# FFN's second projection on one Trainium2 core: product 5 in one row, and the sums for products 6 and 3 on product 7's weight tile

## The chip, the cores and the metric

The kernel runs on one core of one Trainium2 chip. The metric is the device time of one execution in microseconds (us); less is better. A core has these engines, each with its own list of instructions, worked off in order: TensorE (PE, matmuls, with its weight loads as PEld), VectorE (DVE), ScalarE (ACT), GpSimd (POOL) and SyncE (SP). SP and POOL here mostly issue DMA transfers; sixteen DMA engines carry them out. Engines wait for one another through semaphores.

## The reference

A hybrid encoder of two layers works on 512 tokens of 1024 features in float32. Each layer is

```python
x = x + 0.5 * swiglu(rms_norm(x, ffn1_norm[l]), ffn1_w_in[l], ffn1_w_out[l])
x = x + mixer(rms_norm(x, mix_norm[l]), ...)
x = x + 0.5 * swiglu(rms_norm(x, ffn2_norm[l]), ffn2_w_in[l], ffn2_w_out[l])
```

with

```python
def swiglu(x, w_in, w_out):
    gu = x @ w_in
    g, u = jnp.split(gu, 2, axis=-1)
    return (jax.nn.silu(g) * u) @ w_out
```

and a final RMS norm. `w_in` is 1024 x 5632 and `w_out` is 2816 x 1024. The part that matters here is the last line, the FFN's *second projection* `(silu(g) * u) @ w_out`. It runs four times, once in each FFN. The mixer (neighbourhood attention, Fourier mixing, gates) is not touched.

## The kernel before, in words

**Precision.** Every float32 product is three matmuls on rounded operands: high x high, high x low, low x high (`mm3`; L539, L540 and L542 in the FFN). So each weight tile that was loaded is split in two: ACT makes the high part (`whi`, L210, or L205 where the sign turns), then DVE the low part (`wlo`, L213, or L206). The activations are split the same way (`hl`, with `split`, L350 and L351).

**The second projection** is a Strassen-Winograd product. Output, activations and weights are cut in quarters, and seven products (numbered 1 to 7) of half size take the place of eight. The weights' quarters are called a, b, c, d. The activations' columns are worked in three chunks of 3, 4 and 4 column tiles (`CHUNK`, L44). A product of one chunk is a *step*: 18 matmuls in chunk 0, and 24 in chunks 1 and 2. Each step takes two weight tiles of 512 KB, 128 x 1024 (in chunk 0 the second has half the size). Product 1 uses -a, 2 uses b, 5 uses d+c (d loaded, c added), 7 uses c+a, 6 uses d+c+a, 3 uses d+c+a+b, and 4 uses d alone with its partner added. Products 1 and 6 share PSUM banks, as do 7 and 4. When a product has all three chunks, DVE adds the PSUM banks into x (`update`, L820), and ACT sums squares for the next norm (`squares`, L413).

The order before is: 1 in its three chunks, 2 in its three chunks, then 5, 6, 7, 3 chunk by chunk, then 4 in its three chunks. For 6, DVE adds a tile of a to product 5's tile; for 3 it adds a tile of b to the same tile (L182). In the last chunk of the last FFN the sum for 3 is made by an accumulating DMA.

**The weight stream** (class `Stream`) is one list of items for the whole kernel. SP loads a raw tile (L155), up to `FETCH` = 8 items ahead, into nine raw buffers. Where a quarter has a partner, POOL issues an accumulating DMA into the same tile (L165). Splitting runs `AHEAD` = 2 items ahead into three high and three low buffers. SP issues in program order, so a load whose buffer is not free yet holds up what stands behind it. A load that is in `held` has its accumulating DMA put off to a later place in the program.

**The rest around it.** The activations' 16-bit words are turned by DMA transposes on SP (L381, `zt` from `zs`) and joined again on ACT (L394, `joined`). The last block of the FFN's first projection ends right before the second projection starts; its two transposes stand on SP among the first weight loads of the second projection, and `joined` is called after steps 3 and 5. While product 4 runs, the next norm's operands are made by quads: four transposes on TensorE and their copies (L451, L454), then high and low parts (L455, L456). One of these quads, `quad(0, 0)`, is called after step 6.

Of the kernel before, what the change touches and what calls it, by code (L numbers as in the profile page):

```python
# [21 lines left out]
L = 2  # L22
# [11 lines left out]
FIRST = (1, 2, 5, 6, 7, 3, 4)  # L34
FETCH = 8
# [63 lines left out]
def encoder_kernel(  # L99
# [118 lines left out]
    held = {}  # L218

    def stage_items():  # L220
# [5 lines left out]
        def strassen(s, name, idx, sizes, order, dma=False, behind=None, on_chip=False):  # L226
# [34 lines left out]
        def ffn(s):  # L261
# [7 lines left out]
            for order in ((1,), (2,), (5, 6, 7, 3), (4,)):  # L269
                for c in range(3):  # L270
                    summed = s == (L - 1, 2) and c == 2
                    strassen(s, lambda q: "o" + q, c, out_sizes(c), order, summed)

        for l in range(L):
# [18 lines left out]
            for i in range(2):  # L293
                strassen(s, lambda q: "g" + q, i, two, ORDER if i else FIRST, True, on_chip=False)
# [368 lines left out]
    def stage_ffn(norm, nxt, late):  # L663
# [85 lines left out]

        def released(t):  # L750
# [4 lines left out]
            for key in late_sums:  # L755
                waiting, held[key] = held[key], gate
                with tc.issue_after(gate):
                    for raw in waiting:
                        raw.summed()
# [62 lines left out]
        steps = []  # L822
        for c in range(3):
            steps.append((1, c, lambda c=c: part(0, 0, c)))
        for c in range(3):
            steps.append((2, c, lambda c=c: part(1, 0, c)))
        for c in range(3):
            steps.append((5, c, lambda c=c: comb(part(0, 0, c), part(0, 0, c), part(0, 1, c), ALU.subtract)))
            steps.append((6, c, lambda c=c: comb(part(0, 0, c), part(0, 0, c), part(1, 1, c), ALU.add)))
            steps.append((7, c, lambda c=c: comb(part(0, 1, c), part(0, 1, c), part(1, 1, c), ALU.subtract)))  # L830
            steps.append((3, c, lambda c=c: part(1, 1, c)))
        for c in range(3):
            steps.append((4, c, lambda c=c: fourth(c)))
# [9 lines left out]
        def make(i):  # L843
            if i < len(steps) and i not in made:
                m, c, f = steps[i]
                made[i] = hl(f(), c, f"c{m}")
# [149 lines left out]
        for i, (m, c, _) in enumerate(steps):  # L996
# [16 lines left out]
            if i == 3:  # L1013
                turned.reverse()
                joined()
            if i == 5:
# [10 lines left out]
            if i == 6 and not late:  # L1027
# [10 lines left out]
            if m == 4 and c == 1 and late:  # L1038
                for _ in ready:
                    pass  # L1040
            if c < 2:
# [6 lines left out]
            elif m == 5:  # L1048
                update(ps[5], 0, 1, 1)
                update(ps[5], 1, 1, -1)  # L1050
# [5 lines left out]
            elif m == 7:  # L1056
                if late:
                    make(i + 3)
                update(ps[7], 1, 1, 1)
# [1193 lines left out]
```

## Time and profile before

| what | us |
| --- | --- |
| median of 3 runs | 1835.79 |
| lowest and highest of the runs | 1835.3, 1836.54 |
| profiled execution, its own time | 1837.46 |
| span of the profiled execution | 1835.7 |
| PE busy | 1823.8 |
| DVE busy | 1607.2 |
| ACT busy | 1306.2 |
| second projection, product 1 to the end of product 3, the four FFNs | 90.94, 90.69, 90.85, 91.40 |

The span goes from the first to the last instruction of the profiled execution; what lies around it is the rest of that execution's time. A line of a timeline gives the start in us from the span's start, the length, the engine, the source line, the operation, and out<-in with shapes; in square brackets stands the idle time before it, and what released it. "SPq" and "POOLq" are the issuing of DMAs by these engines, not the transfers. Matmul starts give the pitch better than their lengths, since matmuls are pipelined and overlap.

### The profile page before, as it was taken

The page shows a single profiled execution, that of the slowest core. Times are in us where ns is not written, and L with a number is a line of the kernel's source. Part 1 is how long each engine was busy: PE and PEld are TensorE (multiplying, and loading weights), DVE is VectorE, ACT ScalarE, POOL GpSimd, SP SyncE. Part 2 cuts the span into 40 slices and gives each one's busy share as a digit, 9 for nine tenths or more (in the row PEclk, how much of TensorE's full clock was granted, in tenths as well). Part 3 has the DMA queues.
Part 4 walks back from the last instruction along what each step waited for, and adds up shares of the span by engine and source line. Part 5 has one row for each costly group of instructions (what it writes and reads, how often), then busy time and mean ns, then how long its engine had stood idle before and what let it go on. Part 6 is the DMA issues. An engine that isn't in the chain of part 4 may idle for free.

```text
span 1835.7 us, 24504 instructions
## 1 busy us (share of the span) xinstructions
PE 1823.8 (99%) x8766; PEld 1509.6 (82%) x8766; DVE 1607.2 (88%) x1952; ACT 1306.2 (71%) x1771; POOL 179.2 (10%) x219
## 2 busy tenths in 40 slices
PE   9999999999999999999999999999999999999998
PEld 7888888887878888888888888888888788888876
DVE  7878899878989988889998888998789899887898
ACT  6777875667576777787667777766776776777865
POOL 0001011110111010101010100101001111100010
PEclk9999999999999999999999999999999999999999
DMA  9898798963997789879878987998639876988795
GB/s 303 223 237 225 184 274 272 225 175 116 277 221 193 166 233 242 208 201 281 249 194 212 240 212 197 274 296 186 179 134 264 227 190 183 238 212 223 202 272 162
DMA packets 206387, 403.75 MB, mean 220 GB/s; under 512 B 108733, under 2 KB 108893, under 8 KB 206265
## 3 DMA queue, kind: packets, MB, share of 16 engines
q1 hardware_dynamic: 176536, 300.52, 51.0%
q0 software_dynamic: 29296, 101.12, 30.5%
q8 instruction: 69, 1.13, 0.3%
q10 hardware_dynamic: 432, 0.55, 0.1%
q14 instruction: 54, 0.43, 0.1%
HBM read 370.67 MB, written 2.11 MB: 203 GB/s over the span
## 4 chain that ended last, share of the span: by engine, by line
PE 89%; DVE 3%; DMA 3%; issue 2%; ACT 2%; POOL 0%; SPq 0%; DVEq 0%; ACTq 0%; POOLq 0%
PE A L539 10%; PE A L540 10%; PE A L542 10%; PE o L540 7%; PE o L539 7%; PE o L542 7%; PE B L542 5%; PE B L540 5%; PE B L539 5%; PE ps L344 3%; PE ps L345 3%; PE ps L346 2%; PE C L540 2%; PE C L539 2%; PE C L542 2%
## 5 line engine op out<-in xcount | busy, mean ns | idle before, releaser
L213 DVE TENSOR_TENSOR wlo<-raw,whi 128x1024 fp32r<-128x1024 f32 (+1 forms) x534 | 630.8, 1190 | 166.3 <-ACT whi L210 165.8
L210 ACT ACTIVATE whi<-raw 128x1024 fp32r<-128x1024 f32 (+1 forms) x534 | 546.2, 1033 | 265.4 <-DVE raw L182 70.7
L165 POOL DMA_DIRECT2D raw<-in_wst_dram x170 | 148.6, 900 | 1301.7 <-DMA raw<-in_wst_dram 467.6
L182 DVE TENSOR_TENSOR raw<-raw,raw 128x1024 f32<-128x1024 f32 (+1 forms) x148 | 176.1, 1190 | 2.0
L540 PE MATMUL A<-whi,xl 128*128 128x512 f32 x400 | 155.7, 389 | 0.0
L539 PE MATMUL A<-whi,xh 128*128 128x512 f32 x400 | 155.7, 389 | 0.0
L394 ACT ACTIVATE at<-zt 128x1024 uint16<-128x1024 uint16 (+2 forms) x96 | 110.2, 1165 | 12.0 <-DMA zt<-zs 12.0
L542 PE MATMUL A<-wlo,xh 128*128 128x512 f32 x400 | 115.0, 389 | 0.0
L205 ACT ACTIVATE whi<-raw 128x1024 fp32r<-128x1024 f32 (+1 forms) x83 | 85.6, 1036 | 38.7 <-issue 11.3
L206 DVE SCALAR_TENSOR_TENSOR wlo<-raw,whi 128x1024 fp32r<-128x1024 f32 (+1 forms) x83 | 98.6, 1192 | 11.5 <-ACT whi L205 11.5
L542 PEld LDWEIGHTS A<-wlo,xh 128*128 128x128 f32 x400 | 75.1, 188 | 15.6
L540 PEld LDWEIGHTS A<-whi,xl 128*128 128x128 f32 x400 | 75.1, 188 | 15.4
L539 PEld LDWEIGHTS A<-whi,xh 128*128 128x128 f32 x400 | 75.1, 188 | 15.4
L539 PE MATMUL B<-whi,xh 128*128 128x512 f32 x208 | 81.4, 391 | 1.2 <-ACT whi L210 1.1
L540 PE MATMUL B<-whi,xl 128*128 128x512 f32 x208 | 81.0, 390 | 0.0
L540 PE MATMUL C<-whi,xl 128*128 128x512 f32 x208 | 81.0, 389 | 0.0
L539 PE MATMUL C<-whi,xh 128*128 128x512 f32 x208 | 81.0, 389 | 0.0
L794 ACT ACTIVATE th<-sn,rh 128x512 f32<-128x512 f32 x80 | 54.9, 715 | 36.3 <-DVE sn L631 35.5
L375 ACT ACTIVATE zs<-th 128x1024 uint16<-128x1024 uint16 x80 | 79.5, 1043 | 0.9 <-DVE th L801 0.9
L626 ACT ACTIVATE sn<-A 128x512 f32<-128x512 f32 x104 | 59.0, 586 | 27.5 <-PE A L542 27.2
L542 PE MATMUL B<-wlo,xh 128*128 128x512 f32 x208 | 60.2, 391 | 0.2
L542 PE MATMUL C<-wlo,xh 128*128 128x512 f32 x208 | 60.1, 390 | 0.0
(451 smaller groups left out, 4618.7 us busy)
## 6 DMA issues: line engine op xcount, KB each, us to landing
raw<-in_wst_dram SPq DMA_DIRECT2D x468, 512.0 KB, 6.3
raw<-in_wst_dram POOLq DMA_DIRECT2D x180, 512.0 KB, 8.1
bm<-in_bias_dram SPq DMA_DIRECT2D x16, 512.0 KB, 6.2
raw<-in_wst_dram SPq DMA_DIRECT2D x30, 256.0 KB, 5.1
vs<-v SPq DMA_DIRECT2D x24, 128.0 KB, 5.8
x<-in_xin_dram SPq DMA_DIRECT2D x4, 512.0 KB, 10.2
raw<-in_wst_dram POOLq DMA_DIRECT2D x8, 256.0 KB, 8.4
dft<-in_dft_dram POOLq DMA_DIRECT2D x8, 256.0 KB, 6.7
```

Of the source, the lines that this page charges most:

```text
L165: G.dma_start(out=self.t, in_=wst[GRAN_AT[self.plus]][:, 0 : self.n], accum_op=ALU.add)
L182: V.tensor_tensor(self.raw.t, self.raw.t, self.add.t, ALU.add)
L205: S.activation(hi, t, AF.Copy, scale=-1.0)
L206: self.last = V.scalar_tensor_tensor(lo, t, -1.0, hi.bitcast(F32), ALU.mult, ALU.subtract)
L210: S.activation(hi[:, cs], t[:, cs], AF.Copy)
L213: self.last = V.tensor_tensor(lo[:, cs], t[:, cs], hi[:, cs].bitcast(F32), ALU.subtract)
L375: S.activation(s[:, h], words[:, h], AF.Copy)
L394: S.activation(to[:, w], t[:, w], AF.Copy)
L539: PE.matmul(ps, lh, rh, start=start, stop=False, skip_group_check=again)
L540: PE.matmul(ps, ll, rh, start=False, stop=False, skip_group_check=again)
L542: PE.matmul(ps, lh, rl, start=False, stop=stop, skip_group_check=again)
L626: last_snap[0] = S.activation(t[:, b, :], ps[b], AF.Copy)
```

## The change

The order of the steps becomes a table, `OUT`: 1 in three chunks; 2 of chunk 0; 5 in three chunks; 7, 6, 3 of chunk 0; 7, 6, 2, 3 of chunk 1; 7, 6, 2, 3 of chunk 2; 4 in three chunks. The sums for 6 and 3 are now made on product 7's tile: c+a, then + d (from a fresh tile of d), then + b. In chunks 1 and 2 the tile of b that product 2 uses serves the sum for 3 too, so 14 loads fall away (SP has 599 rows for 613); the loads' partner sums by accumulating DMA are as many as before. The accumulating loads of 5's first two tiles are put in `held` and let go after step 0, behind the last low part that was made then. The joining of turned words moves from after steps 3 and 5 to after steps 5 and 8. Product 5's updates of x are made after (5, chunk 2) and (7, chunk 0); product 2's update comes with its last chunk, in the row 7, 6, 2, 3 of chunk 2; and `quad(0, 0)` is called after (3, chunk 2). The operands of the steps become a table of functions, which changes nothing else.

```diff
@@ (constants)
+OUT = (
+    [(c, (1,)) for c in range(3)] + [(0, (2,))] + [(c, (5,)) for c in range(3)]
+    + [(0, (7, 6, 3)), (1, (7, 6, 2, 3)), (2, (7, 6, 2, 3))] + [(c, (4,)) for c in range(3)]
+)
@@ strassen (the weight stream)
-        def strassen(s, name, idx, sizes, order, dma=False, behind=None, on_chip=False):
+        def strassen(s, name, idx, sizes, order, dma=False, behind=None, from_c=False):
...
-                plus = q2 and not (on_chip and q == "c")
-                r[q] = [Raw(key(q, g), n, key(q2, g) if plus else None) for g, n in enumerate(sizes)]
+                r[q] = [Raw(key(q, g), n, key(q2, g) if q2 else None) for g, n in enumerate(sizes)]
...
+                elif from_c and m in (6, 3):
+                    add(c, d2[g] if m == 6 else None if dma else b, then=b.key if dma and m == 6 else None)
                 elif m == 3:
                     add(d, None if dma else b)
...
                 else:
-                    add(c, a if on_chip else None)
+                    add(c)
@@ ffn (the weight stream)
-            for order in ((1,), (2,), (5, 6, 7, 3), (4,)):
-                for c in range(3):
-                    summed = s == (L - 1, 2) and c == 2
-                    strassen(s, lambda q: "o" + q, c, out_sizes(c), order, summed)
+            for c, order in OUT:
+                strassen(s, lambda q: "o" + q, c, out_sizes(c), order, s == (L - 1, 2) and c == 2, from_c=True)
@@ stage_ffn
+        out_sums = [(stage, "od", 0, g) for g in range(2)]
+        held.update({key: [] for key in out_sums})
+
+        def release(gate, keys):
+
+            for key in keys:
                 waiting, held[key] = held[key], gate
                 with tc.issue_after(gate):
                     for raw in waiting:
                         raw.summed()
...
-        steps = []
...
+        steps = [(m, c) for c, order in OUT for m in order]
...
             if i == 0:
                 settle_at()
-            if i == 3:
+            if i == 0:
+                release(ws.items[ws.prepped - 1].last.ins, out_sums)
+            if i == 5:
                 turned.reverse()
                 joined()
-            if i == 5:
+            if i == 8:
                 joined()
...
-            if i == 6 and not late:
+            if (m, c) == (3, 2) and not late:
                 nxt.quad(0, 0)
...
+            if (m, c) == (5, 2):
+                update(ps[5], 0, 1, 1)
+            if (m, c) == (7, 0):
+                update(ps[5], 1, 1, -1)
             if c < 2:
                 continue
...
             elif m == 5:
-                update(ps[5], 0, 1, 1)
-                update(ps[5], 1, 1, -1)
+                pass
```

How the order of the instructions moves is shown at three places. In these rows the line numbers behind L are those of each kernel's own file (in the changed kernel some lines higher by 3 to 10), and the numbers behind a name tell buffers apart.

First, SP at the end of the last FFN's first projection, before (`raw` a weight tile, `zt` the turned words):

```order
L155 DMA raw_2919_15325<-in_wst_dram 128x512
L155 DMA raw_2922_15343<-in_wst_dram 128x1024
L155 DMA raw_2931_15374<-in_wst_dram 128x1024
L155 DMA raw_2934_15392<-in_wst_dram 128x1024
L155 DMA raw_2937_15404<-in_wst_dram 128x1024
L381 DMA_TRANSPOSE zt_2925_15361<-zs_2916_15318 128x16x128
L381 DMA_TRANSPOSE zt_2927_15368<-zs_2926_15365 128x16x128
L155 DMA raw_2940_15422<-in_wst_dram 128x1024
L155 DMA raw_2945_15445<-in_wst_dram 128x512
L155 DMA raw_2948_15464<-in_wst_dram 128x1024
```

and now:

```order
L159 DMA raw_2907_15301<-in_wst_dram 128x512
L159 DMA raw_2910_15319<-in_wst_dram 128x1024
L159 DMA raw_2919_15350<-in_wst_dram 128x512
L159 DMA raw_2922_15368<-in_wst_dram 128x1024
L159 DMA raw_2925_15383<-in_wst_dram 128x1024
L384 DMA_TRANSPOSE zt_2913_15337<-zs_2904_15294 128x16x128
L384 DMA_TRANSPOSE zt_2915_15344<-zs_2914_15341 128x16x128
L159 DMA raw_2928_15402<-in_wst_dram 128x1024
L159 DMA raw_2933_15425<-in_wst_dram 128x1024
L159 DMA raw_2936_15444<-in_wst_dram 128x1024
```

The rows start with the second tile of product 2's chunk 0. Ahead of the two transposes stood the other chunks of product 2, and there now stand product 5's chunks 0 and 1, each tile of which also gets an accumulating DMA on POOL; behind them follow 5's chunk 2 and 7's chunk 0. On POOL the accumulating loads of product 5's chunk 0 are the first of the projection, before and now.

Second, DVE in chunk 0 of the last FFN, where the sums of weights (`raw` from two `raw`), low parts (`wlo`), operands' low parts (`c7l` is product 7's) and updates (`x`) meet, before:

```order
L351 TENSOR_TENSOR c6l_2980_15613<-at_2699_14147,c6h_2979_15612 128x768
L182 TENSOR_TENSOR raw_2940_15422<-raw_2940_15422,raw_2948_15464 128x1024
L213 TENSOR_TENSOR wlo_2977_15592<-raw_2945_15445,whi_2976_15591 128x512
L820 SCALAR_TENSOR_TENSOR x_75<-o2_2953_15488,x_75 128x512
L820 SCALAR_TENSOR_TENSOR x_75<-o2_2954_15489,x_75 128x512
L182 TENSOR_TENSOR raw_2945_15445<-raw_2945_15445,raw_2955_15490 128x512
L213 TENSOR_TENSOR wlo_2987_15628<-raw_2940_15422,whi_2986_15627 128x1024
L351 TENSOR_TENSOR c7l_2992_15658<-at_2684_14063,c7h_2991_15657 128x768
L213 TENSOR_TENSOR wlo_2990_15647<-raw_2945_15445,whi_2989_15646 128x512
L182 TENSOR_TENSOR raw_2940_15422<-raw_2940_15422,raw_2967_15547 128x1024
L213 TENSOR_TENSOR wlo_2995_15664<-raw_2958_15508,whi_2994_15663 128x1024
```

and now:

```order
L354 TENSOR_TENSOR c7l_2969_15587<-at_2672_14039,c7h_2968_15586 128x768
L354 TENSOR_TENSOR c6l_2977_15630<-at_2687_14123,c6h_2976_15629 128x768
L824 TENSOR_TENSOR at_2836_14936<-at_2836_14936,at_2687_14123 128x768
L217 TENSOR_TENSOR wlo_2972_15594<-raw_2936_15444,whi_2971_15593 128x1024
L354 TENSOR_TENSOR c3l_2987_15670<-at_2821_14849,c3h_2986_15669 128x768
L186 TENSOR_TENSOR raw_2936_15444<-raw_2936_15444,raw_2946_15491 128x1024
L217 TENSOR_TENSOR wlo_2975_15612<-raw_2943_15472,whi_2974_15611 128x512
L830 SCALAR_TENSOR_TENSOR x_75<-o5_2951_15508,x_75 128x512
L830 SCALAR_TENSOR_TENSOR x_75<-o5_2952_15509,x_75 128x512
L186 TENSOR_TENSOR raw_2943_15472<-raw_2943_15472,raw_2953_15510 128x512
L217 TENSOR_TENSOR wlo_2982_15640<-raw_2936_15444,whi_2981_15639 128x1024
L830 SCALAR_TENSOR_TENSOR x_75<-o5_2951_15508,x_75 128x512
```

The updates were those of product 2, and are now those of product 5; four of them stand between the sums for 6 and 3. The operands of 7, 6 and 3 stand ahead of the sums.

Third, DVE at product 4 of the second FFN, before (`xl` is a quad's low part for the next norm):

```order
L351 TENSOR_TENSOR c4l_1533_7994<-at_1301_6864,c4h_1532_7993 128x768
L213 TENSOR_TENSOR wlo_1531_7977<-raw_1478_7696,whi_1530_7976 128x1024
L820 SCALAR_TENSOR_TENSOR x_75<-o7_1458_7618,x_75 128x512
L820 SCALAR_TENSOR_TENSOR x_75<-o7_1459_7619,x_75 128x512
L213 TENSOR_TENSOR wlo_1538_8006<-raw_1505_7842,whi_1537_8005 128x1024
L213 TENSOR_TENSOR wlo_1541_8024<-raw_1510_7866,whi_1540_8023 128x512
L351 TENSOR_TENSOR c4l_1543_8041<-at_1357_7165,c4h_1542_8040 128x1024
L820 SCALAR_TENSOR_TENSOR x_75<-o1_1381_7274,x_75 128x512
L820 SCALAR_TENSOR_TENSOR x_75<-o1_1382_7275,x_75 128x512
L820 SCALAR_TENSOR_TENSOR x_75<-o3_1468_7657,x_75 128x512
L820 SCALAR_TENSOR_TENSOR x_75<-o3_1469_7658,x_75 128x512
```

and now:

```order
L830 SCALAR_TENSOR_TENSOR x_75<-o2_1402_7389,x_75 128x512
L217 TENSOR_TENSOR wlo_1525_7971<-raw_1490_7806,whi_1524_7970 128x1024
L824 TENSOR_TENSOR at_1353_7157<-at_1353_7157,at_1187_6250 128x1024
L217 TENSOR_TENSOR wlo_1528_7989<-raw_1495_7830,whi_1527_7988 128x512
L830 SCALAR_TENSOR_TENSOR x_75<-o1_1377_7266,x_75 128x512
L354 TENSOR_TENSOR c4l_1530_8006<-at_1353_7157,c4h_1529_8005 128x1024
L830 SCALAR_TENSOR_TENSOR x_75<-o1_1378_7267,x_75 128x512
L830 SCALAR_TENSOR_TENSOR x_75<-o3_1456_7630,x_75 128x512
L830 SCALAR_TENSOR_TENSOR x_75<-o3_1457_7631,x_75 128x512
L217 TENSOR_TENSOR wlo_1540_8040<-raw_1498_7849,whi_1539_8039 128x1024
L824 TENSOR_TENSOR at_1427_7500<-at_1427_7500,at_1242_6551 128x1024
L459 TENSOR_TENSOR xl_1532_8010<-xr_1533_8011,xh_1531_8009 128x4x256
```

Product 2's update (`o2`) and one more quad's low part now stand among the low parts of the weights, where 7's update stood before; that one comes earlier now.

More of the change, by code (lines that the diff above doesn't have):

```diff
@@ L754, in released @@
             gate = G.dma_start(out=to, in_=t[0:1, 0, 0, 0:32].bitcast(F32)).ins
[L755 to L759, printed above, removed]
+            release(gate, late_sums)
         def joined():
@@ L995, in stage_ffn @@
         ps = {}
-        for i, (m, c, _) in enumerate(steps):
+        for i, (m, c) in enumerate(steps):
             make(i)
@@ L1048, in stage_ffn @@
             elif m == 5:
-                update(ps[5], 0, 1, 1)
-                update(ps[5], 1, 1, -1)
+                pass
+            elif m == 7:
+                if late:
+                    make(i + 3)
+                update(ps[7], 1, 1, 1)
             elif m == 6:
```

34 lines of the change are left out of this document (16 added, 18 removed).

## The prediction, made before the changed kernel was run

> **What bounds the kernel now.** I read the page's busy times first, then the windows of the four second projections, then the timelines of TensorE, VectorE and the two DMA-issuing queues inside them.
>
> From the page, the span, the busy times, and the chain that ended last by engine:
>
> ```profile
> span 1835.7 us, 24504 instructions
> PE 1823.8 (99%) x8766; PEld 1509.6 (82%) x8766; DVE 1607.2 (88%) x1952; ACT 1306.2 (71%) x1771; POOL 179.2 (10%) x219
> PE 89%; DVE 3%; DMA 3%; issue 2%; ACT 2%; POOL 0%; SPq 0%; DVEq 0%; ACTq 0%; POOLq 0%
> ```
>
> TensorE is busy 99% of the span, and the diff leaves its number of matmuls alone. So time can only be gained where matmuls of the second projection start later than the one before them allows. To find that, the pitch first: in the last FFN product 1 starts at 1721.01 and product 2 at 1736.01.
>
> ```profile
> 1721.01 0.39 PE L539 MATMUL o<-whi,c1h 128*128 128x512 f32 x1
> 1736.01 0.39 PE L539 MATMUL o<-whi,c2h 128*128 128x512 f32 x1
> ```
>
> One product is 11 column tiles of 6 matmuls, so 66 matmuls in 15.00 us, 0.2273 us each. The four projections from product 1 to the end of product 3 (columns: stretch, length, busy time and count of PE, PEld, DVE, ACT, POOL for that tile, clock, DMA share, GB/s):
>
> ```profile
> 219.96:310.90 90.94, 90.31 (x397) 74.15 (x397) 7.59 (x12) 0.00 (x0) 1.00 0.94 267
> 811.81:902.50 90.69, 90.06 (x396) 74.26 (x396) 7.67 (x12) 0.00 (x0) 1.00 0.93 263
> 1130.85:1221.70 90.85, 90.22 (x396) 74.11 (x396) 7.58 (x12) 0.00 (x0) 1.00 0.94 265
> 1721.00:1812.40 91.40, 90.68 (x397) 74.08 (x397) 7.60 (x12) 0.00 (x0) 1.00 0.90 250
> L451 PE MATMUL tr<-ident,x 128*128 128x128 f32 x160 | 20.2, 272 | 0.0
> ```
>
> Six products are 396 matmuls, 90.0 us at that pitch. The first three also hold 8 transposes each (about half a matmul's pitch, 1.0 us together), so they lose nothing I can see. The last has none and loses 91.4 - 90.0 = **1.4 us**. That is all there is to gain inside the part that is reordered. Outside it, TensorE's idle time is 1835.7 - 1823.8 = 11.9 us, of which 8.6 us lie behind the end of the last stretch, where the final norm is unchanged:
>
> ```profile
> 1812.40:1827.10 14.70, 14.70 (x67) 12.16 (x65) 14.67 (x27) 7.87 (x16) 0.00 (x0) 1.00 0.01 3
> ```
>
> **The change part by part.**
>
> *Term 1, the stall that goes.* In chunk 1 of product 5 the second weight tile comes late. The timelines of PE, ACT, DVE and POOL there (start, length, a group; in brackets the idle time before it and its releaser):
>
> ```profile
> 1769.10 1.07 PE L542 MATMUL o<-wlo,c5h 128*128 128x512 f32 x4
> 1770.83 0.50 PE L539 MATMUL o<-whi,c5h 128*128 128x512 f32 x1 [0.66 <-ACT whi L210]
> 1769.72 1.06 ACT L210 ACTIVATE whi<-raw 128x1024 fp32r<-128x1024 f32 x1 [4.48 <-DMA raw<-in_wst_dram]
> 1749.64 1.22 DVE L182 TENSOR_TENSOR raw<-raw,raw 128x1024 f32<-128x1024 f32 x1
> 1760.16 0.86 POOL L165 DMA_DIRECT2D raw<-in_wst_dram  x1 [9.36 <-DVE wlo L213]
> ```
>
> Its buffer came free with DVE's sum ending 1750.9, the load landed and the accumulating load went out at 1760.16, and ACT could start only at 1769.72. Four matmuls at pitch end the group that began at 1769.10 at 1770.0; the next begins at 1770.83. With the low part behind it that is the 1.4 us. In the new order this tile sits in a run of nine buffers that free one after another, eight items ahead, so it goes: **-1.4 us**, bounds -1.4 and 0.
>
> *Term 2, product 5's three chunks in a row.* They need six tiles with two transfers each in 15 us, and they start early: after products 1 and 2's chunk 0, 84 matmuls, at 1721.0 + 84 x 0.2273 = 1740.1. SP and POOL of the same place before, with the medians from issue to landing (windows 1735 to 1756, then 1755 to 1775):
>
> ```profile
> 1713.54 10.45 SPq L155 DMA_DIRECT2D raw<-in_wst_dram  x5
> 1724.09 5.48 SPq L381 DMA_TRANSPOSE zt<-zs  x2
> 1729.66 39.19 SPq L155 DMA_DIRECT2D raw<-in_wst_dram  x18
> 1734.38 0.86 POOL L165 DMA_DIRECT2D raw<-in_wst_dram  x1 [50.10 <-DVE c2l L351]
> raw<-in_wst_dram SPq DMA_DIRECT2D x5, 512.0 KB, 5.7
> raw<-in_wst_dram POOLq DMA_DIRECT2D x3, 512.0 KB, 8.3
> raw<-in_wst_dram SPq DMA_DIRECT2D x8, 512.0 KB, 8.2
> raw<-in_wst_dram POOLq DMA_DIRECT2D x3, 512.0 KB, 9.8
> ```
>
> The four tiles of chunks 0 and 1 take the last four of SP's five places before the two transposes, the fourth at its end, 1724.0. A load and an accumulate take 5.7 + 8.3 = 14.0 to 8.2 + 9.8 = 18.0 us, so it is ready at 1738.0 to 1742.0. Chunk 1's second tile is wanted 1740.1 + 18 x 0.2273 + 12 x 0.2273 = 1746.9, less 1.06 for ACT: 1745.8. Nothing is late. POOL, whose queue was empty for 50.10 us, holds up nobody else.
>
> Chunk 2 of product 5 is behind the transposes. Its first load can go at 1729.66, ready 1743.7 to 1747.7; it is wanted at 1740.1 + 42 x 0.2273 - 1.06 = 1748.6. So 1 to 5 us of margin, if the transposes take what they took. But the accumulates are on POOL as early as their loads land, since the "hold" gates on a DVE instruction and moves no other row on POOL. The nearest rows for a transpose beside accumulates (SP's and POOL's timelines of an earlier block, and the same transpose with no accumulate ahead; last, the packets of the window 1685.7 to 1689.2):
>
> ```profile
> 1683.41 0.87 POOL L165 DMA_DIRECT2D raw<-in_wst_dram  x1 [0.43 <-issue]
> 1685.70 4.97 SPq L381 DMA_TRANSPOSE zt<-zs  x1
> 1470.68 1.82 SPq L381 DMA_TRANSPOSE zt<-zs  x1
> q0 software_dynamic: 186, 0.70, 104.3%
> ```
>
> For 3.5 us only the accumulates' queue had packets, then the transpose ran: 4.97 against 1.82, 3.2 us longer. Waiting at both transposes makes SP free 6.3 later and chunk 2's first tile ready at 1750.0 to 1754.0, 1.4 to 5.4 late. But 0.70 MB in 3.5 us is 2.6 us for 512 KB, and the first of the four loads, issued 1715.8, lands near 1721.5; four accumulates one after another end near 1732. So one wait, to 1732 or 1733: ready 1746 to 1751, from 2.6 early to 2.4 late. Bounds 0 and +5.4 per projection. I take **0**: the short end of the landings belongs to the stretch with fewer loads in flight, which this is. The Trainium skill, in "DMA: Bandwidth & Descriptors", section "Queues, rings and completion order", says that each DMA engine takes turns between the queue rows packet by packet. By that rule the transpose would share with the accumulates and Term 2 would be 0 with certainty; the row of 186 packets from one queue alone speaks against it, and the row decides.
>
> *Term 3, VectorE in chunk 0's steps 7, 6, 3.* DVE's timeline gives spacings of 1.13 for 1024 columns, 0.87 for 768, 0.60 for 512:
>
> ```profile
> 1742.49 1.22 DVE L213 TENSOR_TENSOR wlo<-raw,whi 128x1024 fp32r<-128x1024 f32 x1
> 1743.63 0.95 DVE L351 TENSOR_TENSOR c5l<-at,c5h 128x768 fp32r<-128x768 f32 x1
> 1750.78 0.69 DVE L213 TENSOR_TENSOR wlo<-raw,whi 128x512 fp32r<-128x512 f32 x1
> 1751.38 1.28 DVE L820 SCALAR_TENSOR_TENSOR x<-o,x 128x512 f32<-128x512 f32 x2
> ```
>
> Three pairs of low parts 5.2, four sums 3.5, 5's four updates 2.4, three operands' low parts 2.6, a combination 0.9: 14.6 us in 54 matmuls, 12.3 us. So 2.3 us too much, but the operands' parts and the combination (3.5) stand ahead of the sums, in product 5's stretch, which has no sums of weights: 6 low parts 6.3, 2 operands 2.3, 3 combinations 3.4, 12.0 of 15.0. Bounds 0 and +2.2 each, taken **0**. In chunks 1 and 2, steps 7, 6, 2, 3 ask 8 low parts, 4 sums, 4 operands and 2 combinations, 18 x 1.13 = 20.3, of 96 matmuls' 21.8. Product 3's PSUM banks come from product 5, whose updates must end before its first matmul at 1740.1 + 15.0 + 8.2 = 1763.3: they are queued behind 7's first low parts at about 1756 and end by 1761.
>
> *Term 4, the end.* Product 2's update of x and one quad (transposes, copies, a low part) move into the time between chunk 2 and product 4. DVE's busy share by stage, chunk 2 and then product 4 of the second FFN, product 4 of the first and third:
>
> ```profile
> 880.80:902.50 21.70, 21.70 (x97) 17.98 (x96) 21.70 (x24) 12.72 (x17) 0.00 (x0) 1.00 0.77 229
> 902.50:919.30 16.80, 16.80 (x84) 14.10 (x83) 16.80 (x19) 14.25 (x23) 2.59 (x3) 1.00 0.82 226
> 310.90:328.00 17.10, 17.10 (x85) 14.37 (x84) 15.15 (x19) 12.30 (x21) 1.71 (x2) 1.00 0.82 241
> 1221.70:1238.50 16.80, 16.80 (x84) 14.10 (x83) 14.86 (x18) 11.99 (x20) 2.34 (x3) 1.00 0.99 324
> ```
>
> In the second FFN DVE has no idle time left, and +1.13 and +1.2 = 2.3 us come; the first and third have 1.9 idle, 0.4 short. 5's updates (2.4) leave the stretch before, and TensorE was not held in it (21.70 of 21.70 busy). Bounds 0 and +3.1 over all; **0**. The 8 transposes only change place.
>
> *Term 5, fourteen loads fewer* (7.3 MB of the page's 403.75, two products' chunks in four FFNs but for one). Where TensorE waits for no load, as in the windows above but for Term 1, that gives **0**; bounds -2 (nearly all of the 11.9 - 8.6 - 1.4 us of idle left) and 0.
>
> ```profile
> DMA packets 206387, 403.75 MB, mean 220 GB/s; under 512 B 108733, under 2 KB 108893, under 8 KB 206265
> ```
>
> **Sum:** span 1835.7 - 1.4 + 0 + 0 + 0 + 0 = 1834.3. The profiled execution took 1837.46, so it would be 1836.1; the runs' median, 1835.79, is 0.1 above the span, so the median to come is **1834.4**.
>
> **The rivals.**
>
> *(a) The forecast*, 0.60: own range 1833.4 to 1835.7, the latter if Term 1 is not gained.
>
> *(b) Small new waits eat the gain*, 0.20: a low part behind a sum (Term 3) or the end's quad (Term 4). For it speaks DVE's excess of 2.3 us in 12.3 and its 16.80 of 16.80; against it, that these are sums over a stretch that begins with a lead. 0.5 us each in the four and Term 4's half: -1.4 + 2.0 + 1.1 = 1837.5; range 1835.8 to 1839.
>
> *(c) Slower: the transposes wait behind 5's early accumulates*, 0.15. Place: SP, between 5's chunk 1 and chunk 2 tiles. For it: 4.97 against 1.82, and only one queue's packets. Against: it needs late landings too. Price 2.0 us in each of four projections, near the late end of one wait and in the lower half of two: -1.4 + 8.0 = **1842.4**. It decides from (3.7 + 1.4) / 4 = 1.3 us per projection. That the hold does not hold back the accumulates is its condition, not enough by itself: alone it costs nothing, by Term 2's first four tiles.
>
> *(d) Faster than the bound*, 0.05: the freed transfers also shorten waits in the stages behind (Term 5's -2): 1832.4, or a little below.
>
> **How the numbers follow.** A measurement of this kernel tells some 0.2%, 3.7 us, from no change: below 1832.1 is faster, above 1839.5 slower. Faster gets (d), 0.05. Slower gets (c) and a tail of (b), 0.16. The rest, 0.79, is within. The range takes (a), (b), most of (d) and the lower half of (c): 1832.8 to 1841.0.
>
> **What would show it.** Right: the four stretches of the o tile at 91.0 us or less, the last about 90.0; no PE idle above 0.3 us with an ACT or DVE releaser in products 5, 7, 6; the two transposes in the last FFN ending on SP by 1733. Wrong for Term 2: PE idle before 5's chunk 2 or 7's chunk 0, released by ACT after a load, and SP's transposes at 5 us each. Wrong for Term 3: PE idle released by DVE low parts in 6 and 3 of chunk 0. Wrong for Term 4: the second FFN's product 4 longer than 16.80. The forecast fails if one of these is above 1.3 us in each projection.

## The result, and the profile after

| | us |
| --- | --- |
| before, median of 4 runs beside it (1835.3 to 1839.39) | 1836.16 |
| changed, median of 4 runs (1921.35 to 1935.09) | 1924.31 |
| ratio of changed to before | 1.0487, 95% interval 1.0445 to 1.053 |
| changed, profiled execution, its own time and its span | 1925.38, 1923.6 |

The change costs some 88 us, 4.9%. The forecast was 1834.4, and the range ended at 1841.0. From the page of the changed kernel, the same three lines as before:

```profile
span 1923.6 us, 24477 instructions
PE 1852.0 (96%) x8766; PEld 1521.7 (79%) x8766; DVE 1608.3 (84%) x1952; ACT 1308.2 (68%) x1771; POOL 179.2 (9%) x219
PE 81%; DMA 9%; DVE 3%; ACT 3%; issue 3%; SPq 1%; POOL 0%; DVEq 0%; ACTq 0%; POOLq 0%
```

DMA, which held 3% of the chain that ended last, now holds 9%. The four second projections, from product 1 to the end of product 3, in the windows of the o tile (columns as before; the clock is the one after the counts):

```profile
220.25:337.40 117.15, 98.38 (x396) 78.59 (x395) 8.43 (x13) 0.00 (x0) 0.90 0.95 204
838.99:951.80 112.81, 96.13 (x396) 75.68 (x395) 8.07 (x13) 0.00 (x0) 0.94 0.90 198
1181.07:1293.40 112.33, 96.71 (x396) 76.74 (x395) 7.90 (x13) 0.00 (x0) 0.94 0.94 211
1794.20:1900.60 106.40, 97.19 (x397) 78.21 (x397) 8.67 (x14) 0.00 (x0) 0.94 0.89 207
```

Together they last 448.7 us; before they lasted 363.9. So 84.8 of the spans' 87.9 us lie here: 26.2, 22.1, 21.5 and 15.0 in the four, 21.2 in the mean. This sum over the four stretches is the measure for the experiments below, because a profiled execution has it without what differs elsewhere from one execution to the next.

Below, an *accumulate* is an accumulating load. What TensorE waited for in the changed kernel (total, times, longest); then SP's and POOL's timelines at its first projection, which starts at 220.25; last, SP at the same place before, where that projection starts at 219.96:

```profile
PE o L542 <- ACT whi L214: 40.3, 13, 7.4
PE o L543 <- DVE c5l L354: 10.3, 3, 4.7
PE o L545 <- DVE wlo L217: 9.0, 4, 7.6
223.33 21.46 SPq L384 DMA_TRANSPOSE zt<-zs  x2
244.88 38.60 SPq L159 DMA_DIRECT2D raw<-in_wst_dram  x13
218.92 0.86 POOL L169 DMA_DIRECT2D raw<-in_wst_dram  x1 [36.97 <-DVE th L805]
220.70 0.86 POOL L169 DMA_DIRECT2D raw<-in_wst_dram  x1 [0.91 <-DVE th L811]
223.91 0.86 POOL L169 DMA_DIRECT2D raw<-in_wst_dram  x1 [2.35 <-DMA raw<-in_wst_dram]
232.68 0.86 POOL L169 DMA_DIRECT2D raw<-in_wst_dram  x1 [7.90 <-DVE wlo L210]
223.04 6.77 SPq L381 DMA_TRANSPOSE zt<-zs  x2
229.90 1.62 SPq L155 DMA_DIRECT2D raw<-in_wst_dram  x2
```

The hold on chunk 0's two accumulates keeps nothing back: the first goes out at 218.92, before product 1 has begun, and the second at 220.70. Chunk 1's two follow at 223.91 and 232.68, while the transposes are under way. SP stands 21.46 us at the two transposes (before: 6.77), and the load of 5's chunk 2 goes out at 244.88, 24.6 us after the start of product 1. Before, the first load behind the transposes went out 9.9 us after it. The packets of the window 223 to 255, what landed there, and the timelines of ScalarE, VectorE and TensorE:

```profile
q1 hardware_dynamic: 3753, 1.44, 79.9%
q0 software_dynamic: 548, 1.72, 47.5%
DMA packets 4304, 3.20 MB, mean 100 GB/s; under 512 B 3688, under 2 KB 3688, under 8 KB 4301
raw<-in_wst_dram POOLq DMA_DIRECT2D x2, 512.0 KB, 19.8
247.16 2.36 DVE L354 TENSOR_TENSOR c5l<-at,c5h 128x1024 fp32r<-128x1024 f32 x2 [8.20 <-DMA zt<-zs]
258.66 1.34 ACT L397 ACTIVATE at<-zt 128x1024 uint16<-128x1024 uint16 x1 [18.30 <-DMA zt<-zs]
260.95 0.80 PE L542 MATMUL o<-whi,c5h 128*128 128x512 f32 x1 [7.45 <-ACT whi L214]
269.04 1.06 ACT L214 ACTIVATE whi<-raw 128x1024 fp32r<-128x1024 f32 x1 [6.89 <-DMA raw<-in_wst_dram]
```

Both queues (q1 with the transposes and plain loads, q0 with the accumulates) are at work in that window, and their shares add up to over 100%, but together they move only 100 GB/s. The third and fourth accumulate take 14.1 and 25.5 us to land (19.8 is their median), where 8.3 and 9.8 were quoted before. Product 5, whose matmuls last 15.0 us at pitch, takes from 239.3 to 277.6, and 35.5, 35.5 and 27.6 us in the other projections.

The slow transposes reach TensorE in three ways here. VectorE's low operand part `c5l` is released only by the DMA that turns the words: VectorE sits idle 8.20 us before it here, and 6.86 to 11.76 us in the other projections (TensorE's wait: 4.65 us here). ScalarE waits 18.30 us for the turned words before `joined` (L397), and the high part of chunk 1's second tile, whose accumulate lands at 258.21, stands behind that (TensorE's wait: 7.45 us). And chunk 2's loads stand behind the transposes on SP (TensorE's wait: 4.85 us).

### The profile page after: what moved, and what is told of

Same layout as the page of the kernel before. It is cut to its first block, busy times and chain, and to the rows that moved or that the text cites. A ratio compares the mean times of both kernels' runs of the same rounds, so it can differ in the third digit from the quotient of the medians.

```text
span 1923.6 us, 24477 instructions
## 1 busy us (share of the span) xinstructions
PE 1852.0 (96%) x8766; PEld 1521.7 (79%) x8766; DVE 1608.3 (84%) x1952; ACT 1308.2 (68%) x1771; POOL 179.2 (9%) x219
## 4 chain that ended last, share of the span: by engine, by line
PE 81%; DMA 9%; DVE 3%; ACT 3%; issue 3%; SPq 1%; POOL 0%; DVEq 0%; ACTq 0%; POOLq 0%
PE A L542 9%; PE A L543 9%; PE A L545 9%; DMA raw<-in_wst_dram 9%; PE o L542 6%; PE o L543 6%; PE o L545 6%; PE B L545 4%; PE B L542 4%; PE B L543 4%; PE ps L347 2%; PE ps L348 2%; PE ps L349 2%; PE C L543 2%; PE C L542 2%
## 5 line engine op out<-in xcount | busy, mean ns | idle before, releaser
L397 ACT ACTIVATE at<-zt 128x1024 uint16<-128x1024 uint16 (+2 forms) x96 | 110.6, 1165 | 64.2 <-DMA zt<-zs 64.2
L210 DVE SCALAR_TENSOR_TENSOR wlo<-raw,whi 128x1024 fp32r<-128x1024 f32 (+1 forms) x83 | 98.6, 1193 | 11.8 <-ACT whi L209 11.8
L542 PE MATMUL o<-whi,c5h 128*128 128x512 f32 x88 | 43.3, 492 | 36.0 <-ACT whi L214 36.0
```

The lines of the kernel that those rows point to most:

```text
L210: self.last = V.scalar_tensor_tensor(lo, t, -1.0, hi.bitcast(F32), ALU.mult, ALU.subtract)
L397: S.activation(to[:, w], t[:, w], AF.Copy)
L542: PE.matmul(ps, lh, rh, start=start, stop=False, skip_group_check=again)
```

## The experiments

The theory after the result: transposes and accumulating loads in flight together slow each other, SP stands behind the transposes, and product 5's weights come late. Rival 1: three chunks of product 5 in a row ask for more transfers than there are, however they are timed. Rival 2: any traffic of SP's beside the accumulates does it. Rival 3: ScalarE is held up by the joining of the turned words, which now stands ahead of operands.

Beside these runs, the kernel before had medians of 1841 to 1844 us and single runs from 1836 to 1854.

**e1: a hold that holds.** The gate becomes a DMA on POOL that reads the second turned tile:

```diff
-        out_sums = [(stage, "od", 0, g) for g in range(2)]
+        out_sums = [(stage, "od", c, g) for c in range(3) for g in range(2)]
-                release(ws.items[ws.prepped - 1].last.ins, out_sums)
+                released(turned[-1][0], out_sums, 1)
```

> The changed kernel, with the hold on the accumulating loads of product 5 made by a small DMA on GpSimd that reads the second turned tile, so that GpSimd's queue waits until both transposes have landed; product 5's tiles of all three chunks are let go by it. Theory (transposes and accumulates in flight together slow each other, and SP stands behind the transposes): SP's two transposes take 5 to 7 us instead of 20 to 27, no stall above 3 us in product 5, each stretch from product 1 to the end of product 3 at 90 to 94 us, total 1834 to 1845 us. Rival 1 (three chunks of product 5 in a row ask more of the DMA engines than they give in 15 us): the accumulates begin even later, product 5 still takes 30 us or more, total 1890 or above.

Measured: 1878.14 us, ratio 1.0183 (1.0148 to 1.0218). SP, POOL and ScalarE at its first projection, which starts at 219.84:

```profile
222.93 6.71 SPq L384 DMA_TRANSPOSE zt<-zs  x2
234.12 6.19 POOL L169 DMA_DIRECT2D raw<-in_wst_dram  x7
243.66 1.06 ACT L214 ACTIVATE whi<-raw 128x1024 fp32r<-128x1024 f32 x1 [10.92 <-DMA raw<-in_wst_dram]
```

The transposes are back at 6.71 us, and the four stretches last 401.5 us. So the theory explains a good half (448.7 - 401.5 = 47.2 of 84.8), but its forecast of 1834 to 1845 fell. A second cause stands behind the first: the accumulates now go out 14 us after the start of product 1, and land one after another, 2.5 to 4 us apart. The first is 3.2 to 5.7 us late for product 5 in the four projections, and the ones for 7 and 6 are late by up to 1.4 us too. Rival 1 is partly right, though product 5 takes 17 to 19 us and not 30.

**e2: ordinary copies in place of the transposes.** The last block's two transposes become plain DMA copies, so the words are not turned.

```diff
-            turned.append((turned_words(z2), 1, f0))
+            turned.append(((copied_words if jb == NB - 1 else turned_words)(z2), 1, f0))
```

> The changed kernel, with the last block's two DMA transposes in each FFN replaced by ordinary DMA copies of the same 512 KB each on the same queue (the words are not turned, so the result is another one). Theory: it is the transposes that suffer from and slow the accumulates, not any transfer: SP's two copies are issued in about 1 us together, product 5 takes 15 to 18 us, total 1834 to 1845 us. Rival 1 (the row of three chunks asks too much): product 5 still takes 30 us or more, total above 1890. Rival 2 (any traffic on SP beside four accumulates does it): in between, 1860 to 1910.

Measured: 1855.05 us in one execution, above the 1834 to 1845 that were expected. A wait of 7.07 us in it lies in the mixer of the first layer, which is no part of the edit. The four stretches; SP at the two copies; and the packets of the window 223.4 to 240, to be held against the changed kernel's:

```profile
sum 370.16, PE 364.92 PEld 294.81 DVE 31.77 ACT 0.00; mean PE 91.23 PEld 73.70 DVE 7.94 ACT 0.00
223.47 3.95 SPq L747 DMA_DIRECT2D zt<-zs  x2
DMA packets 1506, 5.07 MB, mean 306 GB/s; under 512 B 163, under 2 KB 163, under 8 KB 1503
```

So 448.7 - 370.2 = 78.5 of the 84.8 us hang on these eight DMAs being transposes: with the same accumulates at the same time and the same bytes on SP, the DMA engines move 306 GB/s and not 100, and product 5 takes 15.0 us in the first two FFNs and in the last (15.9 in the third). The copies held SP for 3.95 us, not the 1 us expected. Rivals 1 and 2 fall as the main cause. What is left, 370.2 - 363.9 = 6.3 us, is for the most part waits for weights in products 7 and 6 of chunk 0.

**e3: no accumulates for 5's chunks 0 and 1.** These tiles are loaded as d alone.

```diff
+                alone = from_c and q == "d" and idx < 2
-                r[q] = [Raw(key(q, g), n, key(q2, g) if q2 else None) for g, n in enumerate(sizes)]
+                r[q] = [Raw(key(q, g), n, key(q2, g) if q2 and not alone else None) for g, n in enumerate(sizes)]
```

> The changed kernel, with product 5's tiles of chunks 0 and 1 loaded without their accumulating partner (d in place of d+c; four accumulating DMAs fewer in each FFN, the rest unchanged). Theory: the two transposes take 5 to 7 us, total 1833 to 1842 us. Rival 3 (ScalarE is held up by the joining of turned words, which now stands ahead of product 5's and 7's operands): ScalarE still waits for the turned words and product 5 still stalls by 5 us or more, total above 1855.

Measured: 1833.85 us in one execution. TensorE waits for nothing in the o tile, and the stretches are as short as the pitch allows:

```profile
223.17 6.99 SPq L385 DMA_TRANSPOSE zt<-zs  x2
220.08:309.94 89.86, 89.86 (x396) 74.00 (x395) 7.89 (x13) 0.00 (x0) 1.00 0.85 241
1719.29:1809.07 89.78, 89.78 (x397) 74.27 (x396) 8.14 (x13) 0.00 (x0) 1.00 0.82 225
```

Rival 3 falls as a cause of its own: the joining stands where the change puts it, and nothing waits, so `joined` only passes on what the transposes lose. In this order, the steps, the sums on 7's tile and the moved updates cost nothing by themselves.

**e4: side by side.** A kernel of its own measures the disputed cost, each group started when all before has landed.

> A kernel of its own that leaves the whole encoder out and copies x to the output. One after another, each after all before has landed: two transposes of 512 KB alone; four accumulating loads of 512 KB alone; four loads alone; four accumulates with two transposes; four loads with two transposes behind them; four accumulates with two plain copies; one accumulate with one transpose; two with two; four accumulates with four loads. Theory: two transposes alone 5 to 7 us, four accumulates alone 10 to 12, both together 20 to 27, more than their sum of 16; the loads with transposes near their sum, 10 to 13; accumulates with copies and with loads near their sums too. If instead both together take 16 or less, the slowness in the changed kernel is not of these two alone. Two with two: between 11 and 20.

SP's issue of two transposes alone, and beside four accumulates; POOL's issue of four accumulates alone, and with the transposes; and ScalarE's rows that end the waits, in order of time: for the two transposes alone, for the four accumulates alone, for the second accumulate beside transposes, for all of that group, and for four accumulates with two copies:

```profile
17.15 4.69 SPq L129 DMA_TRANSPOSE zt<-zs  x2
24.02 0.20 ACT L142 ACTIVATE seen<-zt 128x1 f32<-128x1 f32 x1 [2.11 <-DMA zt<-zs]
24.62 3.70 POOL L126 DMA_DIRECT2D raw<-in_wst_dram  x4 [24.18 <-ACT raw L144]
37.64 0.20 ACT L142 ACTIVATE seen<-raw 128x1 f32<-128x1 f32 x1 [2.12 <-DMA raw<-in_wst_dram]
47.94 3.54 POOL L126 DMA_DIRECT2D raw<-in_wst_dram  x4 [19.62 <-ACT raw L144]
48.60 18.65 SPq L129 DMA_TRANSPOSE zt<-zs  x2
64.45 0.20 ACT L142 ACTIVATE seen<-raw 128x1 f32<-128x1 f32 x1 [10.87 <-DMA raw<-in_wst_dram]
71.35 0.20 ACT L142 ACTIVATE seen<-zt 128x1 f32<-128x1 f32 x1 [0.89 <-DMA zt<-zs]
100.78 0.20 ACT L142 ACTIVATE seen<-raw 128x1 f32<-128x1 f32 x1 [2.29 <-DMA raw<-in_wst_dram]
```

Two transposes alone land in 6.9 us (17.15 to 24.0), four accumulates alone in 13.0, both together in 23.4, so 3.5 us more than their sum. The expectation of 20 to 27 held; the 10 to 12 for four accumulates alone did not. The greater harm is in the order of landing: beside each other, the second accumulate lands 16.5 us after the group's start, not 8, and SP is held 18.65 us instead of 4.69. Two with two took 16.6 us, and one with one 7.4. Four loads with two transposes behind them took 12.5 us, four accumulates with two plain copies 15.7. Four accumulates with four loads took 19.7, near the sum of 13.0 and 7.9 alone, and those accumulates landed 3.8 us apart, where alone they landed 2.3 to 2.7 apart.

**e7: two accumulates instead of four**, chunk 1's left out (e3's edit with `idx == 1`).

> The changed kernel with product 5's tiles of chunk 1 loaded without their accumulating partner (d in place of d+c there), so that two accumulating loads instead of four (one of 512 KB, one of 256 KB) go out ahead of and beside the transposes. Theory: the harm goes with the bytes of accumulates in flight: SP's two transposes 8 to 14 us, product 5 stalls by 0 to 6 us, total 1840 to 1870 us. If it is all or nothing: as with four, 20 us and above 1900.

Measured: 1841.64 us in one execution, where the kernel before had 1841.93. The forecast of the total held. The transposes take 9.10, 8.43, 6.84 and 6.89 us, and the stretches 364.8:

```profile
223.14 9.10 SPq L385 DMA_TRANSPOSE zt<-zs  x2
sum 364.81, PE 362.98 PEld 295.26 DVE 32.18 ACT 0.00; mean PE 90.74 PEld 73.82 DVE 8.05 ACT 0.00
```

The first two accumulates are on their way before the transposes are issued (3.1 us after the start of product 1), and in e9, which issues them alike, they land 5.7 and 7.4 us after that start. It is the third and fourth, put out beside the transposes, that cost 448.7 - 364.8 = 83.9 us. (Whether it is their number or their time that counts, e7 alone does not tell.)

**e8: the cause alone, in the kernel before.** Product 2's tiles of chunks 1 and 2 each get an accumulating load of another quarter, in the old order.

```diff
+                if q == "b" and order == (2,) and idx > 0:
+                    r[q] = [Raw(key(q, g), n, key("a", g)) for g, n in enumerate(sizes)]
```

> The kernel before, in its order, with the suspected cause alone added: product 2's tiles of chunks 1 and 2, which are loaded just ahead of the two transposes, each get an accumulating load of another quarter (so the result is another one). Theory: SP's two transposes take 18 to 27 us instead of 5.5, and products 2 and 5 stall by 10 us or more in each projection, total 1885 to 1950 us. If the order of the change is needed for the loss: transposes up to 10 us, total below 1850.

Measured: 1889.85 us in one execution, within the 1885 to 1950 of the theory. SP at the first projection, TensorE's wait in product 2, and the four stretches:

```profile
223.05 20.24 SPq L383 DMA_TRANSPOSE zt<-zs  x2
PE o L541 <- ACT whi L210: 40.6, 4, 12.1
sum 417.14, PE 373.68 PEld 303.04 DVE 30.70 ACT 0.00; mean PE 93.42 PEld 75.76 DVE 7.67 ACT 0.00
```

Four accumulates ahead of and beside the two transposes bring 53 of the 84.8 us without any of the change: the transposes take 14.8 to 20.2 us (18 to 27 were expected), and TensorE waits 8.5 to 12.1 us in product 2 of each projection. All later waits in the projections come to 0.8 us. That the new order, with chunk 2's accumulates next in line, makes the rest of the loss is argued, not shown.

**e9: two free, the others held** on POOL (e1's edit with `c in (1, 2)`).

> The changed kernel, with the accumulating loads of product 5's chunk 0 free as they are, and those of chunks 1 and 2 held on GpSimd's queue by the small DMA that reads the second turned tile. Theory (two accumulates ahead of the transposes cost little, as with chunk 1's left out; four cost 15 us and more on SP; and held ones land 2.6 to 3.2 us apart, wanted 22.1, 24.8, 27.5 and 30.3 us after the start of product 1): SP's two transposes 7 to 9 us, accumulates of chunk 1 go out at 12 to 14 and land by 20, no stall above 1 us in product 5, 0.5 to 2.5 us in 7 and 6 of chunk 0 in each projection; total within 6 us of the kernel before, so some 80 us of the change's loss gone by holding back two of the four. Rival 1 (supply of accumulates is short however they are spread): stalls of 5 us or more in product 5, total 1860 and above.

Measured: 1865.42 us, ratio 1.014 (1.0119 to 1.0162); stretches 390.0. The transposes are at 6.7 to 9.4 us, as expected, but product 5 takes 17.5 to 20.4 us instead of 15.0 (waits of 0.5 to 2.6 us and slower matmuls behind them), and the total is 24 us above the kernel before, not within 6. It lies where rival 1 put it, at 1860 and above, though not with stalls of 5 us. The packets of 234 to 262 there:

```profile
q0 software_dynamic: 922, 2.99, 54.3%
q1 hardware_dynamic: 1571, 4.93, 48.4%
```

The DMA engines are full in that window, half with accumulates and half with loads. The held accumulates land 2.7 to 3.8 us apart, the first of them 24.6 us after the start of product 1, while a product uses a 512 KB tile in 12 x 0.2273 = 2.7 us. So at that pace the accumulates have to run early, and early is where the transposes are. Seen so, both causes are one place: the row of 5s needs its sums before the last block's words are turned.

**e5 and e6: parts of the change.** In e5 product 2 is back in one row behind product 1; in e6 the whole old order is back, and only 7 before 6 and the sums on 7's tile are left.

```diff
 (e5)  [(c, (1,)) for c in range(3)] + [(c, (2,)) for c in range(3)] + [(c, (5,)) for c in range(3)]
       + [(c, (7, 6, 3)) for c in range(3)] + [(c, (4,)) for c in range(3)]
 (e6)  [(c, (1,)) for c in range(3)] + [(c, (2,)) for c in range(3)]
       + [(c, (5, 7, 6, 3)) for c in range(3)] + [(c, (4,)) for c in range(3)]
```

> The changed kernel with one part undone: product 2 in its three chunks right behind product 1, as before; then 5 in three chunks, then 7, 6, 3 chunk by chunk, then 4; the turned words joined after steps 3 and 5 as before. The 14 loads come back. Product 5's accumulating loads now follow the transposes by SP's own order. Theory (two causes: transposes and accumulates in flight together; and accumulates that land one after another at 2.6 to 3.2 us each, so that a row of eight, 5's and 7's first, has to begin some 22 us ahead): transposes 5 to 7 us, the first accumulate goes out 13 to 16 us after the start of product 1 and is wanted at 30, so no stall above 1 us in 5, at most 2 us in 7 and 6 of chunk 0; total within 4 us of the kernel before. Rival 1 (5 in a row asks too much however early it starts): stalls of 3 us or more in each projection, 12 us or more above the kernel before.

> The order of before (1 and 2 in three chunks; 5, 7, 6, 3 chunk by chunk; 4), with one part of the change alone: 7 ahead of 6, and the sums for 6 and 3 made on product 7's tile with a fresh tile of d. As many loads and accumulates as before. Theory: neutral, within 3 us of the kernel before; the last FFN's stall of 1.4 us may go or stay. If the sums on 7's tile were to blame for a part of the loss: stalls in 6 and 3 released by VectorE, more than 1 us in each projection.

Measured: e5 1857.37 us, 1.0088 (1.0068 to 1.0109), stretches 374.4; e6 1849.75 us, 1.0045 (1.0018 to 1.0072), stretches 371.0. Both lie above their forecasts (within 4 and 3 us of the kernel before; measured 15 and 8 us above), and e5's total is in its rival's range. The transposes take 5.3 to 6.8 us in both. A wait that both have is in product 6 of the second chunk; TensorE's row in e6, and VectorE's rows there:

```profile
281.80 0.73 PE L545 MATMUL o<-wlo,c6h 128*128 128x512 f32 x2 [0.96 <-DVE wlo L217]
279.39 1.22 DVE L186 TENSOR_TENSOR raw<-raw,raw 128x1024 f32<-128x1024 f32 x1
280.52 1.22 DVE L217 TENSOR_TENSOR wlo<-raw,whi 128x1024 fp32r<-128x1024 f32 x1
```

A sum stands ahead of the low part that TensorE wants, and VectorE has no gap. So the sums on 7's tile do cost a wait of about 1 us per projection (e6: 4.0 us in four, e5: 4.3) when 7, 6, 3 follow with no product 2 between, much as e6's rival had it. (e5 also waits in 7 and 6 of chunk 0, and e6 once, 2.7 us, in the last FFN's chunk 2, where sums are made by DMA.) Neither beats the kernel before.

**e10 and e11: the sum on VectorE.** Since e3 without accumulates is the fastest, d+c is made by VectorE from a fresh tile of c, in chunks 0 and 1 (e10) or chunk 1 alone (e11):

```diff
-                    add(d)
+                    add(d, Raw(key("c", g), sizes[g]) if from_c and idx < 2 else None)
```

> The changed kernel, with d+c for product 5's chunks 0 and 1 made by VectorE from a fresh tile of c, in place of the accumulating loads; four accumulates fewer and four plain loads more in each projection, the whole computation is done. Theory (transposes beside accumulates, and accumulates that land 3 us and more apart, are the loss): no stall above 1 us in product 5, SP's two transposes 5 to 8 us; VectorE has 4.0 us more to do per projection, in stretches where it has 2 to 3 to spare, so 0 to 2 us of new waits each; total from 4 us below to 8 us above the kernel before. If the row of 5s itself were too much for SP's loads: stalls of 3 us or more in 5, total 1855 and above.

> The same for product 5's chunk 1 alone; chunk 0's two accumulating loads stay, and go out ahead of the transposes as in the changed kernel. Theory: as with chunk 1's accumulates left out (1841.6 us, at that of the kernel before), plus 2.3 us of VectorE per projection in a stretch with 3 to spare: SP's two transposes 7 to 9 us, stalls of 0.5 to 1.5 us in 7 and 6 of chunk 0, total from 2 us below to 8 us above the kernel before.

Measured: e10 1882.07 us, 1.0224 (1.02 to 1.0248), stretches 394.4; e11 1859.95 us, 1.0108 (1.0079 to 1.0136), stretches 378.5. Both missed: they are 41 and 19 us above the kernel before, and their stretches 30.5 and 14.6 us longer. VectorE's sums make low parts late (in e10 TensorE waits 6.3 us in four for `c7l` and 5.3 in eight for `wlo`), and weights are late too (7.5 us in eleven waits for `whi`). For the latter an explanation, not shown, is that the additional tiles take raw buffers, so that fewer items fit ahead; in e10 the first accumulate of product 5, now chunk 2's, goes out 20 us after the start of product 1.

No version that makes the whole sum was found that beats the kernel before.

## Why the prediction was wrong

**Term 1 came out in size, but only where four accumulates are left out.** In e3 the last FFN's stretch is 89.78 us against 91.40, and nothing in it waits. The tile that came late before has no accumulate in e3, so that the order alone would bring it in time is not shown. In e7, which keeps two of the four, that stretch is 90.77.

**Term 2 failed, in two steps.** First, "one wait, to 1732 or 1733": a transpose beside accumulates was priced by 4.97 against 1.82 us, from a place where two accumulates were under way, and the two were taken as one after the other. That was a single row of a mild case; the 3.5 us window with packets of one queue alone was its start. They run side by side, and both crawl: 20.0 to 27.0 us on SP instead of at most 11.8 (5.48 + 6.3), and in the first projection chunk 1's accumulates land 14.1 and 25.5 us after their issue, where four in a row were to take some 10.5 (1721.5 to 1732). So "nothing is late" fell for chunk 1 as well, and the term saw one way only, over SP to chunk 2's loads, where `c5l` on VectorE and `joined` on ScalarE wait for the turned words too. Chunk 2's first tile, loaded from 244.88 on, reached ScalarE at 269.04, 24.2 us later, where 14 to 18 were reckoned from load to landing. The bound of +5.4 per projection was the wrong bound, since it added waits to the transposes and left the accumulates at their pace; 15.0 to 26.2 were measured. e7 (two accumulates) loses 5.3 us against e3 over the four stretches, and the change (four) 89.2, so the cost does not grow in proportion. Second, the margin of chunk 2 was taken from the landing time of one tile, without the queue of accumulates before it, and 7's was not worked out. In e1 and e9, where the transposes take 4.9 to 9.4 us and the accumulates start 14.3 and 14.7 us after product 1 (in the first projection), the stretches are still 38 and 26 us longer than before.

**The hold without effect** was read rightly from the order: in the trace the first accumulate goes out at 218.92, before product 1 has begun. "Alone it costs nothing" was wrong; e1 gains 47 us in the four stretches by a hold that holds.

**The rule of the Trainium skill** ("DMA: Bandwidth & Descriptors", "Queues, rings and completion order"), that each DMA engine takes turns between queue rows, was set aside for one row. It fits these traces better than the row did: in the 23.4 us of e4 the two queues hold 62.6% and 41.2% of the DMA engines' time. The conclusion that was drawn from it, no delay at all, is wrong all the same: side by side, both took longer than alone (23.4 us for the group, against 6.9 and 13.0).

**Rival (c) named the mechanism and the place, SP between 5's chunk 1 and chunk 2 tiles,** and got a chance of 0.15 and a price of 2.0 us per projection, where 21.2 were measured in the mean. Its condition was already seen as met. A hint in the kernel was passed over: the first projection holds its early accumulates behind a POOL DMA that reads a turned tile (`released`, with `late_sums`), which is the hold that e1 uses.

**Terms 3 and 4 held** where nothing else disturbs; Term 5 was not tested by itself. e3 shows no wait in chunk 0. Product 4 of the second FFN is 17.70 us after 16.80, and "longer than 16.80" was to speak against Term 4; but TensorE is busy in all of it, and the 0.9 us are about the 8 transposes of `quad(0, 0)` (1.0 us), which now stand in that stretch:

```profile
951.80:969.50 17.70, 17.70 (x91) 14.97 (x90) 17.70 (x19) 16.62 (x29) 2.60 (x3) 1.00 0.85 233
```

## What to carry to other kernels

When a change moves a DMA of one kind beside another kind, price the pair by a run of the pair, and not by the one row in which they met mildly; and ask what stands behind each on its queue. A hold has to be a wait on the engine that issues what is held, so look in the order of that engine for the row that waits. Margins for a row of transfers are those of the last one in the queue, at the pace of the whole queue, and not the landing time of one.

## What the runs showed of the hardware that was not expected

Transposes and accumulating loads side by side take more than their sum (23.4 us against 6.9 + 13.0), and SP is held for most of it (18.65 us against 4.69), while ordinary copies of the same bytes beside the same accumulates took 15.7. The excess comes with the number: one with one landed in 7.4 us, less than the first of each takes alone (4.6 + 5.4), and two with two in 16.6, more than 6.9 + 8.0. Why the pair is slower than its sum stays open; the packets of both queues were seen to overlap, but not what they wait for.

A stall costs more than its length. The window behind the first stall of the changed kernel, with its first three matmuls, the first of which ends the wait:

```profile
248.40:255.00 6.60, 5.06 (x11) 3.47 (x11) 3.12 (x3) 0.00 (x0) 0.00 (x0) 0.61 1.19 66
248.44 0.80 PE L543 MATMUL o<-whi,c5l 128*128 128x512 f32 x1 [4.65 <-DVE c5l L354]
249.04 0.63 PE L542 MATMUL o<-whi,c5h 128*128 128x512 f32 x1
249.46 0.63 PE L543 MATMUL o<-whi,c5l 128*128 128x512 f32 x1
```

After a wait of 4.65 us the granted clock is 0.61, and matmuls start 0.42 us apart, not 0.2273. Over the four stretches PE is busy 388.4 us for the same matmuls that took 361.3, so about 27 of the 84.8 us are slower matmuls, the rest waiting. The Trainium skill, in "TensorE: Matmul & The Clock Gate", section "HAM oscillation — how this bites in real kernels", warns of gaps above some 3.4 us; the trace agrees, with 4.65 us and a clock of 0.61. Shorter waits did it too: in e9 the clock is 0.61 from 245.8 to 250.0, behind a wait of 2.56 us, so 3.4 us is no safe bound in these runs.
